# A hybrid encoder step whose instruction order is planned in Python: larger attention units, another order of projections, finer waits

## The chip, the cores and the metric

The kernel runs on one core of a Trainium2 chip. The metric is the device time of one execution in microseconds (us); lower is better. A core has TensorE (PE in the profile; its weight loads are PEld), VectorE (DVE), ScalarE (ACT), GpSimd (POOL) and SyncE (SP), which here only issues DMAs. All computing engines share on-chip memory, and PE writes into eight PSUM banks.

## The reference, cut to what matters

One layer over 512 prompt rows (and 32 sample rows that attend to caches), width 1024:

```
z  = rmsnorm(x) @ w_in          # split into qa,ka,va,ga | qb,kb,vb,gb | qm,gm | indexer
oa = band attention (6 heads x 64, learned relative bias)             # "A"
ob = attention over the 128 best keys by an indexer (6 heads x 64)    # "B"
om = attention into 256 memory tokens (4 heads x 64)                  # "M"
y  = rmsnorm(x + concat(oa*silu(ga), ob*silu(gb), om*silu(gm)) @ w_out)
```

The sample rows go through the same three attentions against cached keys and values. Outputs are y for prompt and sample and the new keys and values. Products are taken as three matmuls of split operands (high x high, low x high, high x low).

## The kernel before, in words

**One order, made by a planner.** The whole program is written out once, by Python code that keeps a clock for each engine (class `Line`). Every engine then executes its own instructions strictly in the order in which they were emitted, waiting on semaphores. The *main line* is a chain of generators given to `line.run`; each yields what its next matmuls need, and `line.run` first lets other *tasks* (generators in a heap, ordered by planned time) emit their instructions while the planner thinks that the needed data are not there. `line.until(cond)` emits no main-line work at all: it runs tasks until the condition holds. So a condition that comes late holds back every main-line matmul behind it, and PE then has only what tasks emit.

**The main line** (function `projections`, lists `EARLY` and `LATE` on lines 44 and 45): the indexer's projection, then ka, va, mk, mv in natural layout (four banks each, two for mk and mv), then q and g of A and M as transposed K tiles (`group_t`: 48 matmuls, two banks), then `LATE`: gb0, kb, qb, vb, gb1, gb2. After that the output projection in two halves of its contraction, `out_part(AM)` and `out_part(B)`. Two of the main line's `line.until` matter here, both in `projections`: before gb0 (the first name of group b) it waits for `0 in over`, and before kb for `2 in over`. `over[0]` and `over[2]` are set at the end of the sample rows' attention of A and of M (`sample_a`, `sample_m`, function `sample`), whose keys lie in the buffers that gb0 and kb need (tags "gate1" and "kb").

**The sample rows.** `sample_a` begins when qa0, qa1 and qa2 are all evicted, `sample_m` when qm0 and qm1 are; each is one long chain over DMA, PE, DVE and ACT (scores, softmax, transposes, mix, transposes) and its last step needs all gates of its group (`mix in gated`).

**The prompt's attention.** `attend(i)` takes unit i: it reserves z buffers (`places`, nine in all, `SCORES`), prepares the pair of heads, takes two PSUM banks for each row of its scores (all at once, through `divided` and `room`), scores, exponentiates, normalizes, transposes each z and mixes with the values. The next unit starts when this one has scored. A unit mixes only when all gates of its group are ready. A's units per pair of heads were three: query tiles (0,1), (2), (3), each with two z buffers and two banks. M's unit holds four query tiles, in four z buffers and four banks. B's units are (0,1), (2), (3).

**Filler.** While the indexer's projection runs, `warm` puts 128 x 128 matmuls on constant data where the planner expects PE to wait.

Of the kernel before, what the change touches and what calls it, by code (L numbers as in the profile page):

```python
# [38 lines left out]
SLACK = 1.1  # L39
HOLD = 3.0  # L40
LAG = 0.2
WARM = 0.7

EARLY = ("ka", "va", "mk", "mv", "qa0", "qa1", "qa2", "ga0", "ga1", "ga2", "qm0", "qm1", "gm0", "gm1")
LATE = ("gb0", "kb", "qb", "vb", "gb1", "gb2")


# [380 lines left out]
def hybrid_step(ctx: ExitStack, tc: tile.TileContext, a: dict):  # L428
# [28 lines left out]
    def room(k=1):  # L457

        yield from line.wait(lambda: len(free_banks) >= k)
        while True:  # L460
            t = sorted(pp.free(f"b{b}") for b in free_banks)[k - 1] + 0.4
            if t <= line.now():
                return
            yield t
            yield from line.wait(lambda: len(free_banks) >= k)
# [2 lines left out]
    waiting = []  # L468

    def there(k):  # L470
        return k == 0 or len(free_banks) >= k and sorted(pp.free(f"b{b}") for b in free_banks)[k - 1] + 0.4 <= line.now()

    def divided(k, issue):

# [324 lines left out]
    def x_load():  # L799

        c = len(x_raw)
        yield from ()
        t = (rp.tile([P, 2, N], F32, tag="xr", name="xr", bufs=3) if c < 3 else
             cp.tile([P, 2, N], F32, tag="gate1", name="xr"))
        if c % 2 == 0:
            firsts.append(cp.tile([P, 2, 2, 296], F32, tag=("q0", "gate0")[c // 2], name="raw"))
        raw = firsts[c // 2][:, c % 2]
        for kk in range(2):
            rows = slice((2 * c + kk) * P, (2 * c + kk + 1) * P)
            DMA.dma_start(raw[:, kk, :], w_in[rows, QI:QI + 296])  # L810
            if c == kk == 0:
                DMA.dma_start(gT[0], a["norm_mix_g"])
            DMA.dma_start(t[:, kk, :], a["x_t"][rows, :])
        raws.append(raw)
        x_raw.append(t)

# [90 lines left out]

    def warm(until):
        fill, line.warm = line.warm, None
        while until - line.clk["PE"] > WARM:  # L910
            PE.matmul(idle[:, 0:P], ones, ones, start=True, stop=True)
        line.warm = fill
# [446 lines left out]
    def gate(nm):  # L1359

        m, i = "abm".index(nm[1]), int(nm[2])

        def rest(g):
            yield from line.wait(lambda: ap is not None and left["tg"] > 0)
            left["tg"] -= 1
            yield line.at(g) - 0.2
            t = ap.tile([P, N // 2], F32, tag="tg", name="tg", bufs=2)
            A.activation(t, g, AF.Tanh, scale=0.5)
            yield line.at(t) - 0.2
            if least(g, V, G) is V:  # L1370
                V.scalar_tensor_tensor(g, t, 1.0, g, op0=ALU.add, op1=ALU.mult)
            else:
                G.tensor_tensor(t, t, g, op=ALU.mult)
                G.tensor_tensor(g, t, g, op=ALU.add)
            left["tg"] += 1
            left[m] -= 1
            if left[m] == 0:
                gated.add(m)

        def done(sl, p):  # L1380
            g = gates[m][:, i, sl]
            V.tensor_tensor(g, p, rb[:, sl], op=ALU.mult)
            line.spawn(rest(g))

        return group_t(done)
# [345 lines left out]
    class Masked:  # L1731

        def __init__(self, pair, tiles, subtrahend):
            self.pair, self.sub = pair, subtrahend
            self.parts = []
            self.rows = []
            for t in tiles:
                n = self.keys(t)
                if not self.rows or self.rows[-1] + n > 512:
                    self.rows.append(0)  # L1740
                self.parts.append((t, len(self.rows) - 1, self.rows[-1], n))
                self.rows[-1] += n
            self.sl = slice(tiles[0] * P, (tiles[-1] + 1) * P)
# [90 lines left out]
                give(*sc[r])  # L1834

    units = []
    TILES = ((0,1),(2,),(3,))
    count = {"scored": 0, "turned": 0, "mixed": 0, "done": 0}

    def attend(i):  # L1840

        u = units[i]
        pair = u.pair
        k = 2 * len(u.rows)
        yield from line.wait(lambda: places[0] >= k)
        places[0] -= k
        if pair.q is None:
            yield from line.wait(pair.needs)
            pair.q, pair.k = yield from pair.prep()
        yield line.sure(*pair.q, *pair.k)  # L1850
        sc = yield from divided(k, u.begin)
        count["scored"] += 1
        if i + 1 < len(units):
            line.spawn(attend(i + 1))
        yield from u.score(sc)
        yield from u.norm()
        yield from line.wait(lambda: count["turned"] >= i)
        yield from u.turn()
        count["turned"] += 1
        yield from line.wait(lambda: count["mixed"] >= i and count["done"] >= i - 1 and oT[pair.m] is not None  # L1860
                             and pair.m in gated and (pair.m != 1 or "vb" in over))
        yield line.sure(*(z for r in u.z for z in r))
        o = yield from divided(1, lambda: u.mix(bank()))
        places[0] += k
        count["mixed"] += 1
        yield from pair.finish(o, u.sl)
        count["done"] += 1

    def upto(n):
        return lambda: count["done"] >= n  # L1870

    nbs = {}

# [36 lines left out]
    projections(LATE)  # L1910
    line.until(lambda: 1 in gated and all(n in over and n in news for n in ("kb", "qb", "vb")))
    rox.close()
    line.until(upto(n_am))
    xpx.close()


    ob = pool(ctx, "ob", "left")
    wq.append(pool(ctx, "wq", "left"))
    xr = [ob.tile([P, D], F32, name=f"xr{t}") for t in range(NT - 1)]
    line.until(lambda: xrS)  # L1920
    xr += [cp.tile([P, D], F32, tag="gate2", name="xr3"), xrS[0]]
    for t in range(NT):
        DMA.dma_start(xr[t], a["x_prompt"][t * P:(t + 1) * P, :])
    def sample_b():
        sp = pool(p2, "sp", "right")
        kt = [sp.tile([P, NKS], F32, name="keysB")]
        pts = [cp.tile([P, S], F32, tag=tag, name="ptS") for tag in ("mk", "mv")]
        kt += [ob.tile([P, NKS + (i - 1) * P], F32, name=f"keysB{i}") for i in range(1, 3)]
        for m, t in enumerate(kt):
            DMA.dma_start(t[:, 0:PAST], a["cache_b_k"][m * P:(m + 1) * P, :])  # L1930
        cbv = []

        def values():
            yield from line.wait(lambda: used["done"] >= n_in + 4)
            cbv.extend((yield from load_cache(("gate0", "q0"), 4, a["cache_b_v"])))

        line.spawn(values())
        yield from line.wait(lambda: "choice" in over and all(n in news for n in ("kb", "qb", "vb")))
        z2 = cp.tile([P, NKS], F32, tag="rank", name="z2")
        V.tensor_copy(z2[0:2 * T], ysS[0:2 * T])  # L1940

        yield from room()
        qbS = sp.tile([P, 3, T], F32, name="qbS")
        p = bank()
        for hp in range(3):
            PE.transpose(p[:, hp * T:(hp + 1) * T], news["qb"][:, hp * P:(hp + 1) * P], ident[:T, :T])
        rounded(qbS, p[:, 0:3 * T].rearrange("p (m c) -> p m c", m=3), -0.125)
        give(p)
        yield from sample(1, 6, 8, [t[:, 0:NKS] for t in kt], cbv, qbS, news["kb"], news["vb"],
                          pts + [kt[2][:, NKS:]],  # L1950
                          lambda g0, rows: z2 if g0 else ysS)
# [3 lines left out]
    def out_part(ks, c0, done, order, apart=()):  # L1955

        ws = []
        for t in order:
            halves = 2 if t in apart else 1
            n = 512 // halves  # L1960
            for f0 in range(0, 512, n):
                acc, = take(1)
                o = acc[:, 0:n]
                for i, k in enumerate(ks):
# [2 lines left out]
                    wh, wl = (w[:, 0, f0:f0 + n] for w in ws[i])  # L1967
                    st, en = i == 0, i == len(ks) - 1
                    m, kk = (0, k) if k < 3 else (1, k - 3) if k < 6 else (2, k - 6)
                    h, l = (x[:, kk, t * P:(t + 1) * P] for x in oT[m])  # L1970
                    yield (wh, wl, h, l) + ((acc,) if st else ())
                    PE.matmul(o, h, wh, start=st, stop=False)
# [8 lines left out]

    for c0 in range(0, D, 512):
        line.run(out_part(AM, c0, lambda *_: None, range(NT)))
    line.until(lambda: 1 in over and count["done"] == len(units))
    p2.close()


    fp = pool(ctx, "fp", "left")
    gf = fp.tile([P, D], F32, name="gf")
    DMA.dma_start(gf, a["norm_final_g"].unsqueeze(0).broadcast_to([P, D]))  # L1990
    sq = fp.tile([P, 512], F32, name="sq")
    ss = fp.tile([P, NT + 1, 8], F32, name="ss")

    pieces = [0] * (NT + 1)

    def settle(t, c0, n):
        rows = P if t < NT else T
        x = xr[t][:, c0:c0 + n]
        s_ = ss[:rows, t, :]
        j = pieces[t]  # L2000
        pieces[t] += 1
        new, run, old = s_[:, 2 * j:2 * j + 1], s_[:, 2 * j + 1:2 * j + 2], s_[:, 2 * j - 1:2 * j]
        last = t == NT - 1 and c0 + n == D
        yield line.at(x) - 0.2
# [22 lines left out]
            V.scalar_tensor_tensor(y[:rows, m:D], y[:rows, m:D], run, gf[:rows, m:D], op0=ALU.mult, op1=ALU.mult)  # L2027
        DMA.dma_start(a["y_prompt"][t * P:(t + 1) * P, :] if t < NT else a["y_sample"], y)

    ready.append(True)  # L2030
    for c0 in range(0, D, 512):
        line.run(out_part(B, c0, lambda t, c, n: line.spawn(settle(t, c, n)),
                          range(NT), (NT - 1,) if c0 else ()))
# [67 lines left out]
```

## Time and profile before

| | us |
|---|---|
| median of 3 runs | 357.85 |
| fastest run | 357.41 |
| the profiled execution | 359.29 |
| its span, first to last instruction | 357.3 |
| PE busy (matmuls) | 345.9 |
| PEld busy (weight loads) | 300.9 |
| DVE / ACT / POOL busy | 282.8 / 222.2 / 180.8 |

One of the three runs took 1858.87 us. The granted clock of TensorE is a mean of 0.991 of full speed. Almost every instruction has line 399 (the recording helper), so groups are told apart by the tiles they write and read: `bank<-wh,xTh` is a projection in natural layout, `bank<-xTh,wh` a transposed one, `bank<-k,q` scores, `bank<-ident,z` transposes, `bank<-z,va` a mix. A matmul's end is modelled, so the distance between starts tells more than its length.

### The profile page before, as it was taken

Reading aid. Unit: us, or ns where it says so; the run is one execution under the profiler, and the core shown is the slowest. Engines: PE = TensorE matmul, PEld = TensorE weight load, DVE = VectorE, ACT = ScalarE, POOL = GpSimd, SP = SyncE. Lnnn points to the kernel's source line nnn. Section 1 sums busy time; section 2 is a strip of 40 time slices with the busy share of each in tenths; the row PEclk is TensorE's granted clock in tenths of the full one; section 3 lists DMA queues with packets and bytes.
Section 4 is the critical chain, followed back from the end, with each engine's and each line's share of the span. In section 5 each row is a group of like instructions: output and inputs, shape, how many; then the busy total and the mean of one; then the engine's idle time right before and its main releaser. Section 6 shows DMA issues by size and latency. Waiting matters only on the chain.

```text
span 357.3 us, 7551 instructions
## 1 busy us (share of the span) xinstructions
PE 345.9 (97%) x2730; PEld 300.9 (84%) x2730; DVE 282.8 (79%) x707; ACT 222.2 (62%) x533; POOL 180.8 (51%) x203
## 2 busy tenths in 40 slices
PE   8999899999999999999999999999999999999992
PEld 7979887999998989888889988999998767767681
DVE  3868776789989999989999874879999879552842
ACT  5765776898666797777763666432657677513253
POOL 2468161466455694343765552554239533515453
PEclk9999989999999999999999999999999999999998
DMA  7999351186556233141124034113324924520024
GB/s 231 317 369 346 84 177 61 38 237 167 142 154 247 61 112 83 32 134 48 48 64 121 34 120 147 29 47 88 105 84 130 381 81 150 176 90 2 0 73 176
DMA packets 39604, 46.31 MB, mean 130 GB/s; under 512 B 5360, under 2 KB 32624, under 8 KB 39568
## 3 DMA queue, kind: packets, MB, share of 16 engines
q1 hardware_dynamic: 39568, 45.85, 41.0%
q8 instruction: 21, 0.34, 0.4%
q14 instruction: 15, 0.12, 0.1%
HBM read 39.67 MB, written 6.16 MB: 128 GB/s over the span
## 4 chain that ended last, share of the span: by engine, by line
PE 78%; DMA 8%; DVE 7%; ACT 3%; POOL 2%; issue 1%; SPq 0%; POOLq 0%; DVEq 0%; ACTq 0%
PE bank L399 78%; DMA raw<-in_w_in_dram 3%; DMA nb<-in_bias_p_dram 2%; DMA raw<-in_w_mem_kv_dram 1%; POOL wl L399 1%; DMA cbi<-in_cache_b_kidx_dram 1%; DVE z L399 1%; DVE rot L399 1%; DVE tmpA L399 1%; DMA xr<-in_x_t_dram 1%; DVE ysel L399 1%; DVE m L399 1%; ACT wh L399 1%; DVE bi L399 0%; ACT z L399 0%
## 5 line engine op out<-in xcount | busy, mean ns | idle before, releaser
L399 POOL TENSOR_TENSOR wl<-raw,wh 128x512 fp32r<-128x512 f32 (+1 forms) x69 | 103.9, 1514 | 95.3 <-ACT wh L399 80.8
L399 PE MATMUL bank<-wh,xTh 128*128 128x384 f32 (+1 forms) x184 | 64.7, 352 | 0.9 <-ACT xTh L399 0.7
L399 ACT ACTIVATE wh<-raw 128x512 fp32r<-128x512 f32 (+2 forms) x77 | 50.4, 662 | 24.0 <-PE bank L399 19.8
L399 PE MATMUL bank<-wh,xTl 128*128 128x384 f32 (+1 forms) x184 | 62.4, 339 | 0.0
L399 PE MATMUL bank<-wl,xTh 128*128 128x384 f32 (+1 forms) x184 | 62.3, 339 | 0.0
L399 ACT ACTIVATE z<-z,st 128x128 f32<-128x128 f32 (+3 forms) x80 | 42.8, 553 | 26.6 <-DVE st L399 26.6
L399 PE MATMUL bank<-xTh,wh 128*128 128x272 f32 x208 | 47.0, 307 | 0.0
L399 PE MATMUL bank<-xTl,wh 128*128 128x272 f32 x208 | 43.0, 288 | 0.0
L399 PE MATMUL bank<-xTh,wl 128*128 128x272 f32 x208 | 42.9, 288 | 0.0
L399 PEld LDWEIGHTS bank<-wh,xTh 128*128 128x128 f32 x184 | 35.7, 194 | 3.4 <-ACT xTh L399 1.0
L399 PEld LDWEIGHTS bank<-wh,xTl 128*128 128x128 f32 x184 | 35.8, 194 | 0.5 <-DVE xTl L399 0.3
L399 PEld LDWEIGHTS bank<-wl,xTh 128*128 128x128 f32 x184 | 35.7, 194 | 0.0
L399 PEld LDWEIGHTS bank<-xTh,wh 128*128 128x128 f32 x208 | 32.5, 190 | 3.4 <-issue 2.6
L399 PEld LDWEIGHTS bank<-xTl,wh 128*128 128x128 f32 x208 | 32.6, 188 | 0.0
L399 PEld LDWEIGHTS bank<-xTh,wl 128*128 128x128 f32 x208 | 32.6, 189 | 0.0
L399 DVE MAX8 m<-ysel 128x8 f32<-128x256 f32 (+2 forms) x48 | 26.4, 551 | 0.2
L399 DVE MATCH_REPLACE8 ysel<-m,ysel 128x256 f32<-128x256 f32 (+2 forms) x48 | 26.1, 543 | 0.0
L399 PE MATMUL bank<-ident,z 128*128 128x128 f32 (+1 forms) x162 | 25.2, 273 | 0.6 <-DVE z L399 0.6
L399 PEld LDWEIGHTS bank<-ident,z 128*128 128x128 f32 (+1 forms) x162 | 18.8, 140 | 4.7 <-DVE z L399 1.1
L399 DVE SCALAR_TENSOR_TENSOR ysel<-r,wI,ysel 128x256 f32<-128x256 f32 (+2 forms) x21 | 17.2, 820 | 4.9 <-ACT r L399 4.3
L399 ACT COPY z<-bank 128x512 f32<-128x512 f32 (+2 forms) x29 | 15.0, 522 | 8.5 <-PE bank L399 6.4
L399 ACT ACTIVATE junkS<-ysS,bi 128x1056 int8<-128x1056 f32 x16 | 18.7, 1170 | 2.2 <-DVE bi L399 2.2
(301 smaller groups left out, 793.8 us busy)
## 6 DMA issues: line engine op xcount, KB each, us to landing
raw<-in_w_in_dram SPq DMA_DIRECT2D x20, 384.0 KB, 3.5
raw<-in_w_in_dram SPq DMA_DIRECT2D x26, 256.0 KB, 3.0
raw<-in_w_out_dram SPq DMA_DIRECT2D x16, 256.0 KB, 3.5
xr<-in_x_t_dram SPq DMA_DIRECT2D x8, 272.0 KB, 4.5
nat<-in_x_prompt_dram SPq DMA_DIRECT2D x4, 512.0 KB, 8.3
raw<-in_w_mem_kv_dram SPq DMA_DIRECT2D x8, 256.0 KB, 3.0
xr<-in_x_prompt_dram SPq DMA_DIRECT2D x4, 512.0 KB, 6.9
out_dram<-xr SPq DMA_DIRECT2D x4, 512.0 KB, 2.6
```

The source lines that it names most:

```text
L399: return fn(*args, **kw)
```

## The change

- The first loads put x's rows ahead of the weights' rows in each pair.
- `warm`: fills while the planned gap is over 0.1 us (it was 0.7), and 0.3 us past the planned end.
- A bank counts as free 0.7 us after its last planned use (it was 0.4).
- `EARLY`: ga0 comes ahead of qa2, and gm0 ahead of qm1.
- A unit waits for the gate of its own K tile, not for all gates of its group.
- A's units are the query tiles (0,1,2) and (3): the first has four z buffers and four banks, the second two and two.
- The main line no longer waits for all A and M units before the output projection, nor for the last rows' residual, nor, ahead of `out_part(B)`, for the sample rows' B attention and all units. Instead `out_part` waits, for each query tile and K tile, for the unit that makes it; two spawned tasks, `last_rows` and `final`, do the loads and the release of buffers; `settle` waits for `ready`.

```diff
-WARM = 0.7
+WARM = 0.1
+LATER = 0.3
-EARLY = ("ka", "va", "mk", "mv", "qa0", "qa1", "qa2", "ga0", "ga1", "ga2", "qm0", "qm1", "gm0", "gm1")
+EARLY = ("ka", "va", "mk", "mv", "qa0", "qa1", "ga0", "qa2", "ga1", "ga2", "qm0", "gm0", "qm1", "gm1")
...
-            t = sorted(pp.free(f"b{b}") for b in free_banks)[k - 1] + 0.4
+            t = sorted(pp.free(f"b{b}") for b in free_banks)[k - 1] + 0.7
...
-            DMA.dma_start(raw[:, kk, :], w_in[rows, QI:QI + 296])
             if c == kk == 0:
                 DMA.dma_start(gT[0], a["norm_mix_g"])
             DMA.dma_start(t[:, kk, :], a["x_t"][rows, :])
+            DMA.dma_start(raw[:, kk, :], w_in[rows, QI:QI + 296])
...
         fill, line.warm = line.warm, None
+        until += LATER if until - line.clk["PE"] > WARM else 0
         while until - line.clk["PE"] > WARM:
...
             left[m] -= 1
+            left[m, i] = left.get((m, i), 2) - 1
+            if left[m, i] == 0:
+                gated.add((m, i))
...
-    TILES = ((0,1),(2,),(3,))
+    TILES = ((0, 1, 2), (3,))
...
-                             and pair.m in gated and (pair.m != 1 or "vb" in over))
+                             and (pair.m, pair.hp) in gated and (pair.m != 1 or "vb" in over))
...
         yield from pair.finish(o, u.sl)
+        u.done = True
         count["done"] += 1
...
-    line.until(upto(n_am))
     xpx.close()
...
-    line.until(lambda: xrS)
-    xr += [cp.tile([P, D], F32, tag="gate2", name="xr3"), xrS[0]]
-    for t in range(NT):
+    for t in range(NT - 1):
         DMA.dma_start(xr[t], a["x_prompt"][t * P:(t + 1) * P, :])
+    def last_rows():
+        yield from line.wait(lambda: xrS)
+        xr.extend([cp.tile([P, D], F32, tag="gate2", name="xr3"), xrS[0]])
+        DMA.dma_start(xr[NT - 1], a["x_prompt"][(NT - 1) * P:S, :])
+    line.spawn(last_rows())
...
             for f0 in range(0, 512, n):
+                line.until(lambda: len(xr) > t)
                 acc, = take(1)
...
+                    unit = next(u for u in units if (u.pair.m, u.pair.hp) == (m, kk) and u.sl.start <= t * P < u.sl.stop)
+                    line.until(lambda: unit.done)
...
-    line.until(lambda: 1 in over and count["done"] == len(units))
-    p2.close()
...
+    def final():
+        nonlocal gf, sq, ss
+        yield from line.wait(lambda: 1 in over and count["done"] == len(units))
+        p2.close()
+        fp = pool(ctx, "fp", "left")
+        gf = fp.tile([P, D], F32, name="gf")
+        DMA.dma_start(gf, a["norm_final_g"].unsqueeze(0).broadcast_to([P, D]))
...
+        ready.append(True)
+    line.spawn(final())
...
         pieces[t] += 1
+        yield from line.wait(lambda: ready)
...
-    ready.append(True)
```

## Rows read from the trace of the kernel before

**Rows 1.** The page, its head and part 1: busy us, share of the span, instructions.

```profile
span 357.3 us, 7551 instructions
...
PE 345.9 (97%) x2730; PEld 300.9 (84%) x2730; DVE 282.8 (79%) x707; ACT 222.2 (62%) x533; POOL 180.8 (51%) x203
```

**Rows 2.** Who PE's matmuls waited for: us in total, times, longest.

```profile
PE bank L399 <- DVE ones L399: 1.1, 1, 1.1
PE bank L399 <- ACT ka L399: 0.9, 1, 0.9
...
PE bank L399 <- DVE z L399: 0.6, 1, 0.6
```

**Rows 3.** Stretches: us, then busy PE, PEld, DVE, ACT, POOL (instructions), PEclk, DMA share, GB/s.

```profile
43.80:47.20 3.40, 3.40 (x15) 3.36 (x14) 2.01 (x4) 3.40 (x7) 3.40 (x2) 0.50 0.65 234
...
274.00:317.00 43.00, 42.97 (x409) 30.93 (x409) 33.46 (x93) 26.39 (x75) 19.04 (x22) 1.00 0.59 201
```

**Rows 4.** Timeline of PE, one visit of scores: start us, us, engine, line, what.

```profile
110.41 0.41 PE L399 MATMUL bank<-xTh,wl 128*128 128x272 f32 x2
110.74 0.45 PE L399 MATMUL bank<-k,q 64*128 64x384 f32 x2
...
111.47 0.52 PE L399 MATMUL bank<-xTh,wh 128*128 128x272 f32 x2
```

**Rows 5.** The chain that ended last, its start: start us, us, what.

```profile
1.63 3.00 DMA xr<-in_x_t_dram
...
4.71 0.76 ACT xTh L399
```

**Rows 6.** Timeline of PE at the end of the sample rows' B attention.

```profile
324.52 0.28 PE L399 MATMUL bank<-vbS,keysB 128*32 128x64 f32 x4
325.35 0.27 PE L399 MATMUL bank<-ident,z 64*128 64x64 f32 x1 [0.55 <-DVE z L399]
```

**Rows 7.** Timeline of DVE: the evictions of qa2, ga0, qm1 and gm0.

```profile
103.64 0.79 DVE L399 SCALAR_TENSOR_TENSOR queried<-bank,rb 128x272 f32<-128x272 f32 x2 [0.29 <-PE bank L399]
...
115.89 0.78 DVE L399 TENSOR_TENSOR gate<-bank,rb 128x272 f32<-128x272 f32 x2
...
154.56 0.78 DVE L399 SCALAR_TENSOR_TENSOR queried<-bank,rb 128x272 f32<-128x272 f32 x2
...
167.82 0.78 DVE L399 TENSOR_TENSOR gate<-bank,rb 128x272 f32<-128x272 f32 x2
```

**Rows 8.** Timeline of PE, POOL and DVE: M's sample chain, gm1's gate, both last steps.

```profile
159.24 0.64 PE L399 MATMUL bank<-cacheM,queried 64*32 64x256 f32 x8
...
173.82 0.38 DVE L399 SCALAR_TENSOR_TENSOR oS<-bank,gate 64x32 f32<-64x32 f32 x2
...
180.58 0.27 PE L399 MATMUL bank<-ident,cacheM 128*128 128x128 f32 x1
...
183.93 0.76 POOL L399 TENSOR_TENSOR gate<-tg,gate 128x272 f32<-128x272 f32 x1
...
185.05 0.45 DVE L399 SCALAR_TENSOR_TENSOR oS<-bank,gate 64x64 f32<-64x64 f32 x2
```

**Rows 9.** Timeline of PE: the first matmuls of gb0 and of kb.

```profile
176.93 0.41 PE L399 MATMUL bank<-xTh,wh 128*128 128x272 f32 x2
...
187.66 0.34 PE L399 MATMUL bank<-wh,xTh 128*128 128x384 f32 x1
```

**Rows 10.** Timeline of POOL and PE: M's units prepared and scored; B's queries turned.

```profile
174.75 1.29 POOL L399 TENSOR_TENSOR ql<-queried,q 128x512 fp32r<-128x512 f32 x1
...
196.14 0.39 PE L399 MATMUL bank<-k,q 64*128 64x256 f32 x2
...
217.71 0.28 PE L399 MATMUL bank<-kl,q 64*128 64x256 f32 x2
...
241.49 0.60 PE L399 MATMUL bank<-ident,qb 128*128 128x128 f32 x4
```

**Rows 11.** Who PE's weight loads waited for, its first row.

```profile
PEld bank L399 <- issue: 18.3, 67, 0.8
```

More of the change, by code (lines that the diff above doesn't have):

```diff
@@ L470, in there @@
     def there(k):
-        return k == 0 or len(free_banks) >= k and sorted(pp.free(f"b{b}") for b in free_banks)[k - 1] + 0.4 <= line.now()
+        return k == 0 or len(free_banks) >= k and sorted(pp.free(f"b{b}") for b in free_banks)[k - 1] + 0.7 <= line.now()
     def divided(k, issue):
@@ L1733, in __init__ @@
         def __init__(self, pair, tiles, subtrahend):
-            self.pair, self.sub = pair, subtrahend
+            self.pair, self.sub, self.done = pair, subtrahend, False
             self.parts = []
@@ L1866, in attend @@
         yield from pair.finish(o, u.sl)
+        u.done = True
         count["done"] += 1
-    def upto(n):
-        return lambda: count["done"] >= n
     nbs = {}
@@ L1983, in hybrid_step @@
         line.run(out_part(AM, c0, lambda *_: None, range(NT)))
-    line.until(lambda: 1 in over and count["done"] == len(units))
-    p2.close()
[L1988 to L1992, printed above, removed]
+    gf = sq = ss = None
+    def final():
[5 more added lines that the diff above has]
+        DMA.dma_start(gf, a["norm_final_g"].unsqueeze(0).broadcast_to([P, D]))
+        sq = fp.tile([P, 512], F32, name="sq")
+        ss = fp.tile([P, NT + 1, 8], F32, name="ss")
+        ready.append(True)
+    line.spawn(final())
     pieces = [0] * (NT + 1)
@@ L1998, in settle @@
         x = xr[t][:, c0:c0 + n]
-        s_ = ss[:rows, t, :]
         j = pieces[t]
         pieces[t] += 1
+        yield from line.wait(lambda: ready)
+        s_ = ss[:rows, t, :]
         new, run, old = s_[:, 2 * j:2 * j + 1], s_[:, 2 * j + 1:2 * j + 2], s_[:, 2 * j - 1:2 * j]
```

## The prediction, made before the changed kernel was run

> **What bounds the kernel now.** I read the page first: PE is busy for 345.9 of 357.3 us, no other engine for more than 282.8 [rows 1]. The list of waits says that this is real: PE's matmuls waited for others in only eight groups, from 1.1 us down to 0.2, 4.4 us in all (three of the eight stand in [rows 2]). So time leaves this kernel in two ways only: PE is given less to do between its first and last matmul, or one of those few waits goes. It enters in one way: PE's stream is held up where it is not held up today. The stretches add a cost that the waits don't show: from 43.8 to 47.2 us the granted clock is 0.50, the lower of the two levels, behind the 0.9 us wait for ka's eviction [rows 2, 3]. Fifteen matmuls started there; at the full clock the same 3.4 us would have needed about half, so the stretch lost some 1.5 us.
>
> **The sum** is made against the profiled execution: 359.29 us, of which 357.3 are the span and 2.0 lie around it. It stands 1.4 us above the median of 357.85, so I add the change's terms to the median.
>
> **A's units of three tiles.** Matmuls, transposes and evicted elements stay the same; there are 6 units instead of 9, so 3 fewer visits of scores and 3 fewer of mixes, if each was a visit of its own. A visit of scores starts 0.33 us after the two matmuls of the projection before it, whose pair otherwise takes 0.25, and the first matmul after it is drawn out (0.52 against 0.41 for two) [rows 4]. With the slower first and last pair inside I put a visit at 0.4 us of PE. Upper end: six visits, 2.4 us. Lower end: nothing, because a score and a mix may already share a visit. I take three: **-1.2 us**. Fewer small DVE, ACT and POOL instructions (reciprocal, o, its two halves) cost nothing on the path, since PE covers them.
>
> **Waits at the end.** Today the main line may not begin the last half of the output projection before the sample rows' B attention is through, and PE stood 0.55 us before that attention's last transpose [rows 6]. With waits by unit, output matmuls can lie there: **-0.6 us**, between 0 and -0.8. The removed wait for A and M units was no wait: the last of them are long done when the projections end. Two DMA groups (the last rows, the final gain) are issued from tasks now; they pass nothing on SP that PE needs soon, so nothing.
>
> **First loads and filler.** PE's first real matmul waits for x's first rows: DMA issued at 1.63, landed after 3.00, then ACT until 5.47 [rows 5]. Ahead of the weights it is issued one slot, some 0.45 us, earlier; but the weights' rounding on ACT, done today before x lands, then follows it. **-0.3 us**, between -0.9 (with a warmer clock at the start) and +0.6 (filler that overruns the data).
>
> **The bank rule, 0.4 to 0.7 us**, makes tasks emit later. PE hardly waits for evictions now, so there is little to gain; it may move the ka wait and its slow stretch [rows 2, 3]. Nothing, between -2.4 and +1.
>
> **The order of projections.** This is the term that decides the sign. Moving ga0 ahead of qa2, and gm0 ahead of qm1, delays both sample chains by one slot of the projections: qa2's eviction, at 103.64, goes to where ga0's was, 115.89; qm1's, at 154.56, to where gm0's was, 167.82 [rows 7]. That is 12.3 and 13.3 us. Their DMAs of cached keys and values, issued by SP when the chain begins, move along. Behind these chains stands the main line: gb0 may not be emitted before `over[0]`, kb not before `over[2]`.
> - A's chain ends at 174.2 us, gb0 starts at 176.93 [rows 8, 9]: 2.7 us of slack, plus some 5 us that its first half spends waiting for ga2's gate, which keeps its slot. Of 12.3 us some 4 are left.
> - M's chain starts its scores at 159.24 and turns its result at 180.58, 21.3 us later; its last step waits until 184.7 for gm1's gate on POOL and ends at 185.5; kb starts at 187.66 [rows 8, 9]. Slack: about 4 us inside the chain and 2.2 behind it. Moved by 13.3 us it would end near 194.7, some 7 us after kb could start. A's 4 us lie before that and are part of it.
>
> So the main line is held for some **7 us** between 175 and 195. Behind the wait are kb, qb, vb and everything after. PE still has what tasks emit: units of A, and M's units, which today wait for four free banks until 196.14 though their operands are ready near 176 [rows 10], and find them sooner while no projection holds any. I put that work at 2.5 us, so 4.5 us of PE stay empty: **+4.5 us**. Lower end 0 (the chains' waits for banks and partners shrink while PE is free), upper end 11 (13.3 less the 2.2 behind, nothing put in). It is not given back later, because PE has no other gap of this size.
>
> Rows 3 show what a wait can bring besides itself: the lower clock after the ka wait. A gap of 4.5 us split in two may bring such a stretch, 1.5 us, or none; I leave it in the range. The Trainium skill, page "TensorE: Matmul & The Clock Gate", section "HAM oscillation — how this bites in real kernels", speaks against the change here: PE that waits between bursts falls back to the lower clock each time. By that rule the sum would be 1.5 us higher, 361.8; the trace agrees as far as the ka wait goes.
>
> Sum: -1.2 - 0.6 - 0.3 + 0 + 4.5 = +2.4, so 357.85 + 2.4 = 360.25, **360.0 us** rounded.
>
> **The rivals.**
> 1. *The chains are not late enough.* The sample chains are full of waits for partners, banks and a crowded DVE, and could lose those 7 us. Then only the gains stand: 357.85 - 2.1 = 355.8, and 353.5 if the ka wait and its slow stretch go too. For it: 12.3 and 13.3 us are slots of a schedule that moves itself. Against it: the 21.3 us of M's chain are mostly its own steps. Chance 0.30.
> 2. *The whole delay lands on PE, and it is slower.* The place is the same, in front of gb0 and kb. If the chains move by their full slots with no task work in the gap, kb is 11 us late; with 1.5 us of lower clock and the 2.1 of gains, 357.85 + 11 + 1.5 - 2.1 = 368.3. It counts as slower from 9.3 us of empty PE on. Chance 0.10.
> 3. *Four banks at once.* M's first unit waited some 20 us (176.0 to 196.14) for its four [rows 10]; A's three big units now ask for as many. At 20 us each A would need 60 more. The chain of units went from its second scores at 110.74 to its tenth at 196.14 [rows 4, 10], 10.7 us a step, so three steps fewer save 32; of the 28 left, 24 are covered between M's last scores at 217.7 and B's queries at 241.49 [rows 10]. 4 us stay: with the gains 359.8, and 364 with the main line held as well. For it: those 20 us. Against it: they fell where kb's projection held four banks itself. Chance 0.05.
> 4. *PE is not full.* PEld is busy for 84% only, and for 30.9 of 43 us from 274 to 317 [rows 1, 3]; 18.3 us of its idle time have no releaser but issue [rows 11]. If that were room which finer waits fill, half of the 12 us idle in that stretch, 6 us, would come off besides the gains: 349.8. Against it: PE's matmuls wait for almost nothing there, and much of it are matmuls that load 32 columns. Chance 0.05. The Trainium skill, page "Perfetto Trace Analysis", section "Identifying the Most-Contended Engine", takes this side: not matmul busy time but weight loads' share tells the headroom. The waits of this trace speak against it.
>
> That leaves 0.50 for the forecast, whose own range is 357.5 to 363.5.
>
> **How the numbers follow.** About 2% (7.2 us), to 350.7 and 365.0, is what a measurement of this kernel can tell from no change. Faster than that: rival 4 and a trace of rival 1, 0.05. Slower: rival 2, and 0.02 of rival 3 and of the forecast with a slow clock, 0.12. Within: 0.83. The range, 353.8 to 365.0, leaves out most of rivals 2 and 4 and the best of rival 1.
>
> **What would show each step.** Right, if between 170 and 200 us PE's matmuls show a wait of several us that ends with the sample rows' oS or the first matmul of gb0 or kb, and kb starts after 190. The units: 6 groups of A's mixes, score visits with three sizes in a row, PE's busy time down by 1 to 2 us. The end: no 0.55 us gap before the last transpose, and output matmuls of the second half before it. The first loads: ACT's first xTh before 4.5 us. Wrong, if kb starts near 186 with no gap before it: then rival 1, and I mis-sized what the sample chains lose. If PE waits after 250 us, B is late and rival 3 has it.

## The result, and the profile after

The changed kernel took 355.84 us in the median of 17 runs, the kernel before 358.19 in as many beside it: ratio 0.992, 95% interval [0.9893, 0.9948]. It is faster, by less than 2%, where 360.0 us was forecast. The profiled execution (354.01 us, span 352.2) is its fastest and that of the kernel before (359.29) lies 1.1 us above its median, so the two profiles differ by 5.3 us where the medians differ by 2.3; the times below are medians of several runs.

The page of after and PE's complete list of waits answer to [rows 1, 2]:

```profile
span 352.2 us, 7548 instructions
...
PE 343.6 (98%) x2744; PEld 299.6 (85%) x2744; DVE 278.3 (79%) x705; ACT 221.2 (63%) x528; POOL 179.5 (51%) x197
```

```profile
PE bank L400 <- DVE ones L400: 1.1, 1, 1.1
PE bank L400 <- DVE wl L400: 0.4, 1, 0.4
```

Two waits are left of eight, and the 0.9 us for ka's eviction is gone. To the end of its last matmul PE was idle for 4.5 us before (350.35 less 345.85 busy) and for 1.7 now (345.28 less 343.59). Its last matmul starts 5.1 us earlier (344.88 for 349.95).

The stretch of [rows 3] that had the lower clock, in after (us, then busy PE, PEld, DVE, ACT, POOL, PEclk, DMA share, GB/s), runs at the full one (16 of its 29 matmuls are short ones, `raw,xF`, so the count does not compare the work with the 15 of before):

```profile
43.80:47.20 3.40, 3.40 (x29) 1.98 (x28) 3.29 (x7) 3.37 (x7) 3.25 (x2) 1.00 0.64 231
```

Now the place on which the forecast rested. DVE's evictions of qa2 and qm1, and the last steps of A's and M's sample chains, answer to [rows 7, 8]:

```profile
110.16 0.78 DVE L400 SCALAR_TENSOR_TENSOR queried<-bank,rb 128x272 f32<-128x272 f32 x2
...
155.05 0.78 DVE L400 SCALAR_TENSOR_TENSOR queried<-bank,rb 128x272 f32<-128x272 f32 x2
...
164.02 0.38 DVE L400 SCALAR_TENSOR_TENSOR oS<-bank,gate 64x32 f32<-64x32 f32 x2
...
179.34 0.45 DVE L400 SCALAR_TENSOR_TENSOR oS<-bank,gate 64x64 f32<-64x64 f32 x2
```

PE in after, M's sample scores, gb0's first matmuls, and the start of kb (the `wh,xTh` of 384 columns), for [rows 8, 9]:

```profile
162.79 0.64 PE L400 MATMUL bank<-cacheM,queried 64*32 64x256 f32 x8
...
167.63 0.41 PE L400 MATMUL bank<-xTh,wh 128*128 128x272 f32 x2
...
175.84 0.18 PE L400 MATMUL bank<-bf_ok,over 128*128 128x1 bf16 x1
175.88 0.31 PE L400 MATMUL bank<-ident,cacheM 128*128 128x128 f32 x1
175.94 0.42 PE L400 MATMUL bank<-wh,xTh 128*128 128x384 f32 x1
```

gb0 and kb start 9.3 and 11.7 us earlier than before, not later, with no gap. kb follows the turn of M's result (PE's `bank<-ident,cacheM`, a transpose) within 0.06 us, and the chain's last step, `oS` at 179.34, comes 3.4 us after kb began: `over` holds the order of emission only, kb's matmuls need nothing of `oS`. The gap of [rows 6] is gone too: the sample rows' last transposes at 317.32 stand between matmuls of the output projection, and gb2 ends near 258 us instead of 272.

### The profile page after: what moved, and what is told of

Its sections match the earlier page's. It is cut to its first block, busy times and chain, and to the rows that moved or that the text cites. A ratio compares the mean times of both kernels' runs of the same rounds, so it can differ in the third digit from the quotient of the medians.

```text
span 352.2 us, 7548 instructions
## 1 busy us (share of the span) xinstructions
PE 343.6 (98%) x2744; PEld 299.6 (85%) x2744; DVE 278.3 (79%) x705; ACT 221.2 (63%) x528; POOL 179.5 (51%) x197
## 4 chain that ended last, share of the span: by engine, by line
PE 95%; DMA 1%; POOL 1%; SPq 1%; DVE 1%; issue 0%; ACT 0%; POOLq 0%; DVEq 0%; ACTq 0%
PE bank L400 95%; DMA xr<-in_x_t_dram 1%; SPq L400 1%; DVE xr L400 0%; POOL xr L400 0%; POOL ss L400 0%; ACT sq L400 0%; POOLq L2106 0%; DVE wl L400 0%; DVEq L400 0%; ACTq L400 0%
## 5 line engine op out<-in xcount | busy, mean ns | idle before, releaser
L400 POOL TENSOR_TENSOR wl<-raw,wh 128x512 fp32r<-128x512 f32 (+1 forms) x69 | 105.4, 1537 | 80.0 <-ACT wh L400 73.9
L400 PE MATMUL bank<-wh,xTh 128*128 128x384 f32 (+1 forms) x184 | 63.8, 347 | 0.0
L400 PE MATMUL bank<-wh,xTl 128*128 128x384 f32 (+1 forms) x184 | 61.2, 332 | 0.0
L400 ACT ACTIVATE z<-z,st 128x384 f32<-128x384 f32 (+3 forms) x80 | 42.4, 549 | 22.9 <-DVE st L400 22.7
L400 PE MATMUL bank<-xTh,wh 128*128 128x272 f32 x208 | 46.1, 303 | 0.0
L400 PEld LDWEIGHTS bank<-wh,xTh 128*128 128x128 f32 x184 | 34.9, 189 | 2.7 <-issue 2.0
L400 PEld LDWEIGHTS bank<-wl,xTh 128*128 128x128 f32 x184 | 34.7, 189 | 1.0 <-DVE wl L400 0.7
L400 PEld LDWEIGHTS bank<-wh,xTl 128*128 128x128 f32 x184 | 34.8, 189 | 0.0
L400 ACT COPY z<-bank 128x384 f32<-128x384 f32 (+2 forms) x26 | 13.2, 511 | 9.6 <-PE bank L400 8.5
L400 POOL TENSOR_TENSOR oBl<-o,oBh 128x128 fp32r<-128x128 f32 (+1 forms) x9 | 5.2, 577 | 27.1 <-ACT oBh L400 27.1
```

Source lines behind the costliest of these rows:

```text
L400: return fn(*args, **kw)
```

## The experiments

All ratios are to the kernel before on the same chip. First the table, then the runs in groups; each was expected to do what stands under its name.

| kernel | edit | median us | ratio, interval |
|---|---|---|---|
| u_start | after, old first loads and filler | 357.1 | 0.9947 [0.9924, 0.997] |
| u_loads | after, old first loads | 357.36 | 0.9954 [0.9933, 0.9975] |
| u_warm | after, old filler | 354.96 | 0.9898 [0.9874, 0.9923] |
| u_order | after, old order of projections | 355.09 | 0.9899 [0.9875, 0.9923] |
| u_tiles | after, old units | 356.97 | 0.9951 [0.9935, 0.9968] |
| u_end | after, old waits at the end | 355.67 | 0.992 [0.9892, 0.9948] |
| u_bank | after, bank rule 0.4 | 360.25 | 1.0053 [1.0034, 1.0072] |
| u_bank55 | after, bank rule 0.55 | 367.15 | 1.0246 [1.022, 1.0272] |
| u_bank85 | after, bank rule 0.85 | 361.6 | 1.009 [1.0066, 1.0115] |
| h_late | after, M's sample chain held back | 364.38 | 1.0155 [1.0112, 1.0198] |
| a_order | before, new order alone | 358.84 | 1.0008 [0.9983, 1.0033] |
| a_bank | before, bank rule 0.7 alone | 361.49 | 1.0084 [1.0055, 1.0114] |
| a_loads | before, new first loads alone | 358.78 | 1.0004 [0.9988, 1.002] |
| a_tilesordergate | before, new units, order, gates | 363.51 | 1.0127 [1.0101, 1.0153] |
| b_parts | before, new first loads, units, gates | 424.34 | 1.1845 [1.1807, 1.1882] |
| b_fixed | b_parts, one planner line mended | 359.62 | 1.0034 [1.0009, 1.0059] |
| b_orderwarm | after, old order and old filler | 364.15 | 1.0165 [1.0132, 1.0198] |
| u_fixed | after, the same line mended | 355.21 | 0.9897 [0.9867, 0.9928] |

**The order of projections: undone in after, done alone in before, and the feared lateness made by hand.**

```
u_order:  EARLY as before (qa2 ahead of ga0, qm1 ahead of gm0)
a_order:  EARLY as after, nothing else
h_late, in sample_m:
- yield from line.wait(lambda: all(n in over for n in ("qm0", "qm1", "mk", "mv")))
+ yield from line.wait(lambda: 2 in gated and all(n in over for n in ("qm0", "qm1", "mk", "mv")))
```

u_order: 

> The changed kernel with the old order of projections (all q of a group, then all gates), units still waiting by K tile. Theory (the sample chains are never late, because the big units took PE work out of the stretch ahead of them): no gap before gb0 or kb in either order, time within 1 us of 355.8. Rival (the new order gives gains by letting units mix sooner): slower, 357 to 358, with A's mixes later. Rival (my forecast: the order costs): faster, below 354.5.

a_order: 

> The kernel before with the order of the early projections of after (ga0 ahead of qa2, gm0 ahead of qm1) and nothing else. Theory (the slots of this order cost little, since both sample chains have slack of other kinds): ratio 0.997 to 1.005, no wait of over 1 us on PE before gb0 or kb. Rival, the step of the prediction taken alone: kb starts at 190 us or later, PE waits some 4.5 us before it, ratio 1.010 to 1.03.

h_late: 

> The kernel after, except that the masked sample row's attention may start its scores only when both gates of A's third group of rows are done too, which holds that chain back by some 20 us: the lateness that the prediction feared, made by hand. Theory of the prediction (a late chain holds the main line in front of kb, and PE runs empty there): kb starts at 190 us or later instead of 175.9, a wait of several us stands before it on PE, the time is 361 to 370. Rival (tasks fill whatever the main line leaves, so lateness is priced only by what no task can fill): kb late, but PE's matmuls wait less than 3 us there and the time is 356 to 359.

a_order decides about the step. There the slots do move. qa2's eviction comes at 115.97, where the forecast put it, and still A's last step comes at 172.27, 1.6 us earlier than in [rows 8]. For M, DVE's eviction of qm1 and the chain's last step (the `oS`):

```profile
163.12 0.78 DVE L399 SCALAR_TENSOR_TENSOR queried<-bank,rb 128x272 f32<-128x272 f32 x2
...
182.53 0.45 DVE L399 SCALAR_TENSOR_TENSOR oS<-bank,gate 64x64 f32<-64x64 f32 x2
```

PE in the same kernel, M's sample scores, its last turn, and kb:

```profile
168.02 0.64 PE L399 MATMUL bank<-cacheM,queried 64*32 64x256 f32 x8
...
181.86 0.27 PE L399 MATMUL bank<-ident,cacheM 128*128 128x128 f32 x1
...
186.27 0.34 PE L399 MATMUL bank<-wh,xTh 128*128 128x384 f32 x1
```

qm1 comes 8.6 us later than in [rows 7] and the scores 8.8 later, yet the chain ends 2.5 us earlier (182.53 for 185.05) and kb starts 1.4 earlier (186.27 for 187.66). From scores to last turn it took 13.8 us instead of the 21.3 of [rows 8]; in after 13.1 (162.79 to 175.88). Its own rival, a wait of 4.5 us before kb, did not come, and the time is that of before. In u_order, with the old order, kb starts at 172.85, 3.1 us earlier than in after; PE waits before it in neither, and the times can't be told apart.

h_late makes the chain really late (`2 in gated` stands for M's own gates, not for A's as its expectation says): its scores come 10.7 us later than in after. PE there:

```profile
172.13 0.41 PE L400 MATMUL bank<-xTh,wl 128*128 128x272 f32 x2
173.45 0.64 PE L400 MATMUL bank<-cacheM,queried 64*32 64x256 f32 x8 [0.91 <-DMA cacheM<-in_cache_mem_k_dram]
...
177.26 0.51 PE L400 MATMUL bank<-kl,q 64*128 64x384 f32 x2
179.07 0.62 PE L400 MATMUL bank<-ident,cacheM 128*128 128x128 f32 x2 [1.31 <-DVE cacheM L400]
180.16 0.65 PE L400 MATMUL bank<-cacheM 128*32 128x64 f32 x16 [0.46 <-ACT cacheM L400]
...
182.32 0.47 PE L400 MATMUL bank<-ident,cacheM 128*128 128x128 f32 x1
182.44 0.67 PE L400 MATMUL bank<-wh,xTh 128*128 128x384 f32 x1
```

And its stretches:

```profile
172.00:178.00 6.00, 4.85 (x44) 3.46 (x42) 4.54 (x14) 0.96 (x4) 1.81 (x1) 1.00 0.27 77
178.00:186.00 8.00, 6.46 (x36) 5.15 (x37) 7.82 (x28) 4.93 (x18) 3.90 (x5) 0.57 0.00 0
```

Here the forecast's picture is complete: the chain's steps are broken by three waits of 2.7 us in all (the idle time of the two stretches: 14 less 4.85 and 6.46), and then the mean granted clock is 0.57, near the lower of its two levels (0.50, 1.2 GHz), from 178 to 186. kb is 6.5 us late, and 364.38 against 355.84 is 8.5 us. kb came at 182.4, before the 190 expected, because the hold was 10.7 us and not 20, and because the chain from scores to last turn shrank once more, to 8.9 us. So lateness is priced as forecast, and more; it did not arise. The Trainium skill ("TensorE: Matmul & The Clock Gate", "HAM oscillation — how this bites in real kernels") shows PE falling back to the lower clock behind waits of several us; here the waits ahead of it were of 0.9 and 1.3 us.

**The start.**

```
u_start: u_loads and u_warm together
u_loads, a_loads (the other way round):  raw rows issued ahead of gT[0] and x's rows
u_warm:  WARM = 0.7, without  until += LATER if until - line.clk["PE"] > WARM else 0
```

u_start: 

> The changed kernel with the weights' rows ahead of x's rows again in each first load, and the old filler rule. Theory (the bank rule took the ka wait away): the first real matmul moves by less than 0.5 us, no ka wait, 355.5 to 356.5. Rival (the first loads took it away): the ka wait and the half clock come back, 358 to 359.

u_loads: 

> The kernel after with the old order of the first loads (a chunk's weight rows ahead of x's rows) and the new filler rule. Tells which half of the start took the wait for ka's eviction and its stretch at the lower clock away. Theory (the loads did, since x's rounding is done earlier): the ka wait of about 1 us and the half-clock stretch at 44 us are back, qa0 starts near 83 us, time 357. Rival (the filler did): no ka wait, qa0 near 80.5, 355.8 to 356.1.

u_warm: 

> The kernel after with the old filler rule (filler matmuls while PE is more than 0.7 us early, no 0.3 us added) and the new order of the first loads. Theory (the loads took the ka wait away): no ka wait, qa0 near 80.5 us, 355.8 to 356.1. Rival (the filler did): the ka wait and the half-clock stretch back, qa0 near 83, 357.

a_loads: 

> The kernel before with the order of the first loads of after (x's rows ahead of a chunk's weight rows) and nothing else. Theory (the loads take away the wait for ka's eviction or the half-clock stretch behind it, as they did in after, where undoing them cost 1.5 us): ratio 0.993 to 0.998, the first index matmul no later, the wait before ka's transposes or its half clock smaller. Rival (they help only beside other parts, or the gain falls to how the plan comes out): ratio 0.999 to 1.01, with new waits after 170 us.

In u_start PE waits for ka's eviction again, ahead of the transposes:

```profile
41.58 0.34 PE L399 MATMUL bank<-wl,xTh 128*128 128x384 f32 x1
43.38 1.37 PE L399 MATMUL bank<-identR,stk 32*128 32x32 f32 x11 [1.47 <-ACT ka L399]
```

and the clock behind them is 0.66 over 43 to 48 us. From there on its plan, the order that the planner wrote, is that of after, shifted: A's scores at 106.6, 113.3 and 140.8 for 103.6, 110.3 and 137.8, the last matmul at 347.68 for 344.88. u_loads does much the same with a wait of 1.1 us. So the first loads alone took that wait and its clock away in the profiled executions: 2.8 us by the spans (355.0 for 352.2). By the medians undoing them costs 1.3 and 1.5 us, by the ratios 1.0 and 1.2, with intervals that overlap after's. How: in after eight of the twenty transposes of that group stand inside ka's projection (four at 35.8, four at 38.3 us), and the other twelve follow on 18 matmuls of va's. With the old loads all twenty stand together behind 12 matmuls of va's, and there PE waits.

The lower clock doesn't follow that wait each time. a_bank has it before the same transposes (0.84 us at 42.04), and its stretch shows the full clock where [rows 3] has 0.50:

```profile
43.80:47.20 3.40, 3.40 (x30) 2.73 (x32) 2.01 (x4) 3.40 (x7) 3.40 (x2) 1.00 0.65 234
```

The executions of one kernel seem to differ in the same way. Seven of u_start's twelve have a mean granted clock of 0.985 to 0.991 and a median of 357.6 us; the other five, at 0.994 to 0.997, have 355.6, about after's time. In u_loads it is six (357.6) and six (356.1). Of the 97 executions of the kernel before that were taken beside the experiments, 34 lie at 0.988 to 0.992 (median 359.7) and 63 above (358.2). The profiled one, at 0.991, is of the first kind; the median of 358.19 is like the second. Where an execution lost its clock was seen in the profiled ones alone.

u_warm fits neither expectation: its wait (2.2 us, for `stk` on DVE, with a clock of 0.71 from 40 to 45) makes qa0 3.4 us later than in after, and the time is still no longer. Its plan differs from then on. a_loads gains nothing in before: its ka wait turns into one of 1.1 us for `stk`, with the lower clock behind it.

**Units, end, gates.**

```
u_tiles:  TILES = ((0,1),(2,),(3,))
u_end:  + line.until(lambda: count["done"] >= n_am)   + line.until(lambda: len(xr) > NT)   + line.until(lambda: ready)
```

u_tiles: 

> The changed kernel with A's units of (0,1), (2), (3) again. Theory (three units fewer are worth 1 to 2 us of visits): 356.8 to 358, eleven or so visits of scores and mixes of A instead of twelve, PE busy up by 1 us; and more of A's work lies ahead of gb0, so the first matmul of gb0 comes 3 us or more later than 167.6. Rival (the units are worth nothing, the gain is all ahead of 65 us): 355.5 to 356.5.

u_end: 

> The kernel after with the three waits of the main line at the end put back (for all of A's and M's units, for the last rows' place, for the end of sample row B and the final gain's place). Theory: +0.6 us over after, 356.4, with a gap of about half a us before the last transpose of sample row B. Rival: nothing, 355.8, since the gap only moves; second rival: the freedom also let the line run earlier, +2 us or more.

u_tiles is 1.1 us slower than after by median (the intervals overlap), but hardly on PE: 343.8 us busy for 343.6, last matmul 0.6 us later. The rest is the tail behind PE's last matmul, 9.3 us for 7.3. u_end brings the 0.55 us gap of [rows 6] back and another that the forecast had put at nothing: 1.27 us at 261.8, behind gb2, where the main line waits again for the last of M's units. PE's last matmul is 1.3 us later, and the median is that of after; with intervals of about 1 us each way neither 0 nor 0.6 is ruled out. The gates by K tile were not undone alone.

**The bank rule, at four values and in before.**

```
t = sorted(pp.free(f"b{b}") for b in free_banks)[k - 1] + 0.4   # 0.55, 0.7, 0.85; the same in there(k)
```

u_bank: 

> The changed kernel with a bank counted free 0.4 us after its last use again. Theory (the bank rule took the wait for ka's eviction and the slow clock behind it away): the wait of about 1 us near 41 us and a stretch at the half clock come back, the projection of va ends 3 us later, the time is 358 to 359. Rival (the first loads did it): no such wait, 355 to 356.5. Rival (nothing in particular, every edit reshuffles the order): anything from 354 to 359 without that wait.

a_bank: 

> The kernel before with the bank rule of after (a bank counts as free 0.7 us after its release instead of 0.4) and nothing else. Theory (the rule is worth some 4 us by itself, since tasks that find a bank too early make PE wait on evictions): ratio 0.986 to 0.991. Rival (the 4.4 us that it made within the kernel after belong to units of three tiles, which want more banks at once, or to a plan that happened to come out badly): ratio 0.996 to 1.004.

u_bank55: 

> The kernel after with 0.55 us in the bank rule in place of 0.7. With 0.4 it took 360.25. Theory (a mechanism: the later a bank counts as free, the fewer matmuls wait on evictions): between the two, 357 to 359, with PE's waits after 250 us between those of the two. Rival (no mechanism, each value reshuffles the plan and its time falls where it falls within some 4 us): outside 357 to 359.

u_bank85: 

> The kernel after with 0.85 us in the bank rule in place of 0.7. Theory (a mechanism, with its gain used up at 0.7, where PE waits 1.3 us in all): 355 to 356.5. Rival (each value reshuffles the plan): outside that, up to 360, by waits in the late part that the other values don't have.

360.25, 367.15, 355.84 and 361.6 us at 0.4, 0.55, 0.7 and 0.85: no trend. Alone in before 0.7 costs 0.84%. There is no ka wait in u_bank, so the rule had not removed it. Each value makes another plan; these are the places where the plans part:

| in the kernel | 0.4 | 0.55 | 0.7 (after) | 0.85 |
|---|---|---|---|---|
| gb2's last matmul, us | 271.1 | 289.2 | 258.4 | 279.0 |
| sample rows' last output matmuls | 336.9 | 350.8 | 321.4 | 346.1 |
| PE's last matmul | 350.7 | 351.7 | 344.9 | 349.0 |
| from there to the end | 7.3 | 13.0 | 7.3 | 10.8 |

In u_bank55, the slowest, two places can be named. The first is M's sample chain in front of kb. PE there:

```profile
176.23 0.43 PE L400 MATMUL bank<-cacheM 128*32 128x64 f32 x16
178.49 0.39 PE L400 MATMUL bank<-ident,cacheM 128*128 128x128 f32 x1 [1.82 <-ACT cacheM L400]
178.57 0.63 PE L400 MATMUL bank<-wh,xTh 128*128 128x384 f32 x1
```

with a granted clock of 0.58 from 178 to 182: h_late's kind of loss, by accident. The second is the end. The sample rows' output (PE, `raw,oS`) comes last but three matmuls:

```profile
349.46 1.92 PE L400 MATMUL bank<-raw,oS 128*32 128x512 f32 x16
351.32 0.38 PE L400 MATMUL bank<-wh,oBh 128*128 128x256 f32 x1
```

and their sums, norm and store follow when PE has nothing left (all engines, `xrS`):

```profile
355.58 3.56 DVE L400 TENSOR_TENSOR xrS<-bank,xrS 32x512 f32<-32x512 f32 x5
...
359.24 0.63 ACT L400 ACTIVATE sq<-xrS 32x512 f32<-32x512 f32 x1 [2.21 <-DVE ss L400]
...
361.68 0.33 SPq L400 DMA_DIRECT2D out_dram<-xrS  x1
```

In after that store is issued at 337.5, 7.4 us before PE's last matmul. What 0.4 and 0.85 lose on the way was not traced to single places.

**Do the gains add?**

```
a_tilesordergate, b_parts:  + left[m, i] ... gated.add((m, i));  (pair.m, pair.hp) in gated;  TILES = ((0, 1, 2), (3,))
b_parts also:  x's rows ahead of raw's;   a_tilesordergate also:  EARLY as after
b_orderwarm:  u_order and u_warm together
b_fixed, u_fixed, in divided:
             if not there(k):
-                yield from room(k)
+                yield line.soon()
                 continue
```

a_tilesordergate: 

> The kernel before with A's units of three tiles and one, the order of the early projections and the gates awaited one K tile at a time; loads, filler, bank rule and end as before. Theory (units worth 1.1 us, order and gates about nothing): ratio 0.995 to 0.999, the ka wait and the half-clock stretch still there. Rival of the prediction (the order costs 4.5 us): ratio 1.005 to 1.015 with kb at 190 us or later. Rival of the scatter: outside both, with waits somewhere else.

b_parts: 

> The kernel before with only the two parts that the runs so far show to gain: the order of the first loads, and A's units of three tiles and one with gates by K tile. Order of projections, bank rule, filler and end as before. Theory (gains add): 0.4 to 0.8 per cent faster than before, 355.8 to 357.2. Rival (scatter): up to 4 us above that, by waits after 100 us on PE.

b_orderwarm: 

> The kernel after without the two parts whose undoing gained some 0.7 us each: the old order of the projections and the old filler rule. Theory (they add): ratio 0.985 to 0.989, 353.4 to 354.7, faster than both kernels. Rival (neither was worth its 0.7 us by itself, both are scatter): 0.990 or more, up to 1.00.

b_fixed: 

> b_parts, with the planner's loop for work that shares a visit changed in one line: a job that finds too few banks looks again a quarter of a us later, and so leaves when a partner has issued it, instead of waiting inside for banks that it already holds. Theory (that trap is the 65 us): A's second unit is read within 6 us of its scores, and the time is 354 to 361. Rival (four banks are missing for another reason, such as the projections and the sample chain holding the rest): the scores are still held for tens of us, and the time stays over 380.

u_fixed: 

> The kernel after with the same one line changed. There no unit's scores lay longer than 3.1 us before they were read, so the trap cost it little: theory 354 to 357.5, that is, after's time within what a shifted plan brings. Rival (units of after lose time in the trap where it does not show as a long hold): below 354, with A's and M's units done earlier than in after (M's second scores before 235 us).

They don't. a_tilesordergate is slower, among other things, by a wait of 1.72 us at 324 us, in the sample rows' B attention, with a clock of 0.59 over 324 to 332; kb starts at 178.9, 8.7 us earlier than in before, so it isn't the place that the forecast named. b_orderwarm waits 1.86 us for a piece of `w_out` at 278 us, with a clock of 0.50 from 280 to 284. Undoing two parts whose undoing alone cost nothing made it some 2.5% slower than after (1.0165 for 0.992).

b_parts is a case of its own. A's second unit of three tiles wrote its scores on PE at 150.5 to 151.7 us:

```profile
151.67 0.33 PE L399 MATMUL bank<-kl,q 64*128 64x384 f32 x2
```

and DVE read the first of them 123 us later:

```profile
274.76 0.28 DVE L399 CUSTOM_DVE_ANT_0 z<-bank,nb 128x128 f32<-128x128 f32 x1
```

Meanwhile it held four of eight banks and no other unit ran. The main line went on nearly alone (75.9 us from kb's start to gb1's, 66.9 in before), and the units' work came behind it (stretches; DVE idle for 46 of the 89 us):

```profile
185.00:230.00 45.00, 41.32 (x225) 36.63 (x225) 16.40 (x31) 7.42 (x10) 19.19 (x14) 0.95 0.22 71
230.00:274.00 44.00, 36.15 (x200) 34.26 (x198) 26.29 (x42) 7.20 (x13) 16.02 (x13) 0.81 0.27 80
```

With no unit to fill in, M's sample chain showed PE's longest wait, 8.5 us before its turn at 182.89. The code gives the cause: in `divided`, a unit that is waiting in `room(4)` can have its scores issued by a partner, and then goes on waiting for four more free banks, with four in its own hands. With the line mended, the same unit is read at once (DVE in b_fixed; its last pair of score matmuls started at 149.70):

```profile
149.55 0.29 DVE L399 CUSTOM_DVE_ANT_0 z<-bank,nb 128x128 f32<-128x128 f32 x1
```

and the time is 359.62: 65 us were that trap. In u_fixed, whose plan stays after's, the mended line changes nothing that can be measured. Units of three tiles open the trap to A, because they take four banks where A's old units took two.

u_order, u_warm and u_fixed at 0.990 lie within the intervals of after's 0.992; none is shown to beat it.

## Why the prediction was wrong

- **The step that failed** is the order of projections: "delays both sample chains by one slot of the projections", so the main line "is held for some 7 us", +4.5. Twice wrong. In after the delay itself hardly came: qm1's eviction was at 155.05 (154.56 before, 167.82 forecast), qa2's at 110.16 (103.64 and 115.89), since the line reached those places earlier (qa0 began at 80.35 for 83.56, the ninth of these projections at 145.17 for 155.06). And where the slots did move, in a_order, by 12.3 and 8.6 us, the chains absorbed it: of the 21.3 us of M's I counted 4 as slack, but 13.8, 13.1 and 8.9 us (a_order, after, h_late) show that at least 12.4 were waiting. So kb was never held, and the +4.5 fell to nothing. The span of a chain that shares DVE and PE with tasks is not its length. The order's own cost is too small to be measured: a_order 1.0008 [0.9983, 1.0033].
- **What stood behind the step** was right: a held main line is not filled, and it brought the lower clock (h_late, u_bank55).
- **The first loads**, -0.3, look mis-sized: undoing them costs 1.0 to 1.5, though not clear of noise, and 2.8 between the profiled executions. I looked at PE's first matmul, which gained 0.18 us, and not at the ka wait and its lower clock, which I had read and left to the bank rule as "may move".
- **The bank rule**, 0 with ends -2.4 and +1: the ends were too near. Against 0.4 it is worth 4.4 us in after, and it costs 3.0 in before (0.84% of 358.8).
- **Units**, -1.2: the time fits (u_tiles, 1.1), which is luck, for the mechanism doesn't: PE was spared 0.2 us of work and the tail 2 us. With another plan in u_tiles, the price of three visits stays open.
- **The end**, -0.6: the gap went as forecast, and no gain can be measured (u_end). That the wait for A's and M's units "was no wait" held in before; in after's plan it would be one of 1.27 us.
- **Rival 1** named the reason, chains that are not late enough, and the time (355.8); that it fits to 0.1 us is luck, since none of its three gains came as it was worked out. **Rival 2** is h_late: its 368.3 against 364.38. **Rival 3** took the right suspect, four banks at once, but it struck in b_parts and not in after, and in another form: not units that queue up, but one that holds what it waits for. In after A's units are slower (third pair scored at 172.1 and 184.1) and nothing waits for them. **Rival 4** fell: PEld is idle as before, 18.1 us of it with no releaser but issue, for 18.3 in [rows 11].
- **What no case had** is the scatter of the plan: a constant moved by 0.15 us moved the time by 6 to 11 us. Of the 2.3 us gained, one source was seen in its place, the wait for ka and the lower clock behind it, which the first loads removed. How much of the 2.3 that makes is open, since most executions of before seem to lack the lower clock; the rest is not assigned to a part, since edits that reshuffle the plan move as much.

## What to carry to other kernels

When a planner writes the order, price a part by what it removes in a traced place, and give the forecast a scatter of its own: try the constants next to the one chosen before a gain is put down to a rule. A chain's slack is its span less the sum of its own steps, not the gap behind it. Whoever waits for several of a scarce thing must not be able to wait while it already holds them.

## What the runs showed of the hardware

One wait of about 1 to 2 us on PE could be followed by a granted clock near the lower level over the next 3 to 8 us: 1.47 us (u_start), 1.82 (u_bank55), 1.72 (a_tilesordergate), 1.86 (b_orderwarm). The stretch lost about as much again as the wait, or up to twice that (4 us at 0.58 lose 1.7, 8 us at 0.59 lose 3.3).

The length of the wait doesn't decide it. 0.85 us ahead of the transposes brought the lower clock in before, 0.84 us at the same place brought none in a_bank. u_bank waited 1.16 us at 274 us and kept the full clock, and so did b_fixed (PE, then its stretch) after 1.77 us:

```profile
39.07 0.82 PE L399 MATMUL bank<-identR,stk 32*128 32x32 f32 x8 [1.77 <-DVE stk L399]
```

```profile
40.00:48.00 8.00, 7.74 (x56) 6.02 (x56) 6.53 (x16) 7.87 (x17) 3.89 (x3) 1.00 0.31 108
```

What does decide it stays open here.
